# Eight of eleven pairs through seven products of sums in the down projection, and weight sums by accumulating transfers

## The chip, the cores and the metric

The kernel runs on one core of a Trainium2 chip. The metric is the device time of one execution in microseconds (us), smaller is better; of the kernel before there are three runs, with a median of 1926.14 us (1925.88 to 1926.17).

## The reference

The program is a trunk of two encoder layers on x of 512 tokens by 1024 channels, in float32. Each layer is a half-weighted SwiGLU feed-forward block (FFN), a mixer of four attention groups, and a second such FFN, each followed by a residual sum and a layer norm.

```python
def _swiglu(h, w_gu, w_down):
    gate, up = jnp.split(h @ w_gu, 2, axis=-1)
    return (jax.nn.silu(gate) * up) @ w_down

for l in range(DEPTH):                      # DEPTH = 2
    x = _layer_norm(alpha * x + 0.5 * _swiglu(x, ffn_w_gu[l, 0], ffn_w_down[l, 0]), ...)
    mix = _token_mixers(x, ...)
    x = _layer_norm(alpha * x + mix, ...)
    x = _layer_norm(alpha * x + 0.5 * _swiglu(x, ffn_w_gu[l, 1], ffn_w_down[l, 1]), ...)
```

The hidden width D_FF is 2816, so gate and up together are a 1024 x 5632 matrix and the down projection is 2816 x 1024. The change touches the FFN alone, which runs four times.

## The kernel before

**Float32 by three matmuls.** TensorE (PE) multiplies numbers rounded to a shorter format (fp32r). Each operand is therefore split into a high half (a cast, on ScalarE, ACT) and a low half (operand minus high half, on VectorE, DVE). Each product then takes three matmuls: high by high, high by low, low by high. In the names, `wh` and `wl` are the halves of weights, `al` those of the input, `dh` and `hh`/`hl` those of hidden values. So each weight tile costs a cast on ACT and a subtraction on DVE (line 405 for gate/up, line 542 for the down weights, line 239 for whole rows of down weights).

**Gate and up by seven products.** The hidden width is cut into 11 pairs of 256 columns. For each pair the product of x (tokens in two halves, channels in two halves) with the weights (channels in two halves, gate and up) is a 2 x 2 by 2 x 2 block product, and it is computed with seven block products of sums, not eight of blocks (class `Pair`). Step names go by product: 1, 2, 5, 6, 7, 3, 4, in this order. The four 512 KB weight tiles of a pair are b11, b21, b12, b22 (first digit: channel half; second: gate or up). DVE forms the weight sums in place: line 458 b11 += b12 (step 5), line 468 b11 + b22 (step 6), line 476 b12 += b22 (step 7), line 491 b21 += that of step 6 (step 4). Each product is 24 matmuls of 256 columns into the banks ga, gb, gc. The results of the activation, h0 (tokens 0 to 255) and h1 (256 to 511), stay in SBUF.

**Down projection by seven products.** Class `Unit` takes two pairs at a time, for which the down weights are four blocks d11, d21, d12, d22 (first digit: pair; second: half of the output columns), each two tiles of 256 KB. It also does seven products, in the order 1, 2, 5, 3, 6, 7, 4, each 12 matmuls of 512 columns into the banks da, db, dc. After each, DVE adds the two banks to x (line 556). Sums of weights are formed on DVE (line 524, two operations of 512 columns each), and so are sums of h (lines 569, 574, 575, 581). `UNITS` says how many units there are: three, so six pairs. Their 21 steps are interleaved with the gate/up steps of pairs 3 to 10 of the program.

**The other pairs directly.** The ten 128-row chunks of the remaining five pairs are multiplied directly, 24 matmuls of 512 columns for each chunk, into eight `acc` banks. The last four chunks (`TAIL`) go token block by token block, so that the layer norm of one block runs beside the matmuls of the next.

**Queues and buffers.** All loads are issued by SP in one queue (line 96). POOL (GpSimd) has no work in the FFN but a power in the layer norm (line 334). A scheduling layer (Tile) orders the instructions of each engine, so the order of a queue isn't that of the code. Weight halves have four buffers each (`WB`); the tiles of down weights have ten (`hl`).

Of the kernel before, what the change touches and what calls it, by code (L numbers as in the profile page):

```python
# [15 lines left out]
ALU = mybir.AluOpType  # L16
AX = mybir.AxisListType
PSUM = bass.MemoryType.PSUM
P = 128
DM = 1024  # L20
S = 512
NT = S // P
DEPTH = 2
FF = 2816
NC = FF // P
# [5 lines left out]
FD = DM // 2  # L31
# [42 lines left out]
def tile_encoder(ctx: ExitStack, tc: tile.TileContext, d: dict, out: bass.AP):  # L74
    nc = tc.nc
    ve, se, ge, te = nc.vector, nc.scalar, nc.gpsimd, nc.tensor

    def pool(name, bufs=1, **kw):
        return ctx.enter_context(tc.tile_pool(name=name, bufs=bufs, **kw))

    cst, st, raw, whi, wlo, blk, sm = (pool("cst"), pool("state"), pool("raw"), pool("whi"), pool("wlo"),
                                       pool("blk"), pool("small"))
    ps = pool("ps", 2, space=PSUM)
    RAW, WB = 3, 4
    BUFS = {"v": 8, "st": 8, "kr": 1, "hl": 10, "nat": 4, "tb": 3, "o": 2, "od": 1, "o2": 2, "p": 6, "oT": 8}
    NPT = 4
    LAG = 3

# [9 lines left out]
    def block(tag, name, dt=F32, width=512):  # L98
        return blk.tile([P, width], dt, tag=tag, name=name, bufs=BUFS[tag])

# [141 lines left out]
    def unit_rows(src, lo=None):  # L242
        r = raw.tile([P, DM], F32, tag="r", name="wr", bufs=RAW)
        load(r, src)
        return wsplit(r, DM, lambda a: a, lo)
# [16 lines left out]
    def cols_of(w):  # L262
        return w.rearrange("(k p) f -> p k f", p=P)

    def mm(o, a, b, start, stop, **kw):
        te.matmul(o, a, b, start=start, stop=stop, **kw)  # L266
        n = 1
        for w in b.shape[1:]:
            n *= w
        pe[0] += n / 2400.0  # L270
# [98 lines left out]

    HTAGS = ["oT"] * 4 + ["nat"] * 2 + ["tb"] + ["v"] * 2 + ["oT"] * 2  # L370
    PARTS = {6: "p", 7: "oT", 8: "p", 9: "nat", 10: "v"}
    UNITS = 3
    TMP = ["o", "o", "od", "o2", "o2", "kr"]

    def ffn(l, f, last, to_next, early=("p", "nat")):
        wgu = cols_of(d["ffn_w_gu"][l, f])
        wd = d["ffn_w_down"][l, f]
        ring = {"raw": 0, "tmp": 0}
        v3 = lambda t: t.rearrange("p (c t) -> p c t", c=2)
# [2 lines left out]
        def raw_tile(name):  # L382

            ring["raw"] += 1
            if ring["raw"] % 7 in (1, 3, 5):
                return raw.tile([P, DM], F32, tag="r", name=name, bufs=RAW)
            return blk.tile([P, DM], F32, tag="pt", name=name, bufs=NPT)
# [5 lines left out]
        def parts4(r, early=None):  # L393

            if early is None:
                h = whi.tile([P, DM], F32R, tag="h", name="wh", bufs=WB)
                lo = wlo.tile([P, DM], F32R, tag="l", name="wl", bufs=WB)
                pieces = [(h, lo, 0, 4)]
            else:
                pieces = [(block(early, "we", F32R), block(early, "we", F32R), k0, 2) for k0 in (0, 2)]  # L400
            out_ = []
            for h, lo, k0, nk in pieces:
                q = slice(k0 * 256, (k0 + nk) * 256)
                se.copy(h, r[:, q])  # L404
                ve.tensor_tensor(lo, r[:, q], h.bitcast(F32), op=ALU.subtract)  # L405
                out_.append(tuple(w.rearrange("p (k c) -> p k c", c=256) for w in (h, lo)) + (k0, nk))
            return out_

        def product(n, o, w, first):

            for c in range(2):
                seq = []
                for h, lo, k0, nk in w:
                    for k in range(nk):
                        seq += [(h, k, k0 + k, "h"), (h, k, k0 + k, "l")]
                for h, lo, k0, nk in w:
                    for k in range(nk):
                        seq.append((lo, k, k0 + k, "h"))
                for m, (a, k, kk, hl) in enumerate(seq):
                    mm(o[:, c], a[:, k, c * P:(c + 1) * P], alk(n, hl, kk), first and c == 0 and m == 0,  # L420
                       c == 1 and m == len(seq) - 1, skip_group_check=True)

        class Pair:
# [6 lines left out]
            def load(self, ns=(11, 21, 12, 22)):  # L430
                j = self.j
                for n in ns:
                    k, u = n // 10 - 1, n % 10 - 1
                    self.r[n] = raw_tile(f"b{n}")
                    load(self.r[n].rearrange("p (k c) -> p k c", k=4),
                         wgu[:, 4 * k:4 * k + 4, u * FF + j * 256:u * FF + (j + 1) * 256])
                return self

            def bank(self, tag, name):
                return bank(tag, name).rearrange("p (c t) -> p c t", c=2)  # L440
# [32 lines left out]

            def step7(self):
                r = self.r
                ve.tensor_tensor(r[12], r[12], r[22], op=ALU.add)
                w = parts4(r[12])
                product(7, self.a, w, False)

                ve.tensor_tensor(self.p5, self.a, self.p5, op=ALU.add)  # L480
# [25 lines left out]
        class Unit:  # L506
# [6 lines left out]
            def load(self):  # L513
                for n, k, u in ((11, 0, 0), (21, 1, 0), (12, 0, 1), (22, 1, 1)):
                    self.r[n] = []
                    for q in range(2):
                        r = block("hl", "d")
                        c = 2 * (self.j + k) + q
                        load(r, wd[c * P:(c + 1) * P, u * FD:(u + 1) * FD])
                        self.r[n].append(r)  # L520
# [37 lines left out]
            def steps(self):  # L558
                (h11, h21), (h12, h22) = (tuple(t.rearrange("p c t -> p (c t)") for t in H[self.j + k]) for k in range(2))
                two = lambda tags, name: [bank(t, name) for t in tags]  # L560
                self.load()
                a = two(("pt", "pt"), "da")
                self.step(1, h11, -1.0, 11, a, True, (0, 0, -1.0))
                yield
                b = two(("pv", "pj"), "db")
                self.step(2, h12, -1.0, 21, b, True, (0, 0, -1.0))
                yield
                t = block("tb", "dt")
                ve.tensor_tensor(t, h21, h22, op=ALU.subtract)
                self.add(11, 12)  # L570
                c = two(("pv", "pj"), "dc")
                self.step(5, t, 1.0, 11, c, True, (1, 1, 1.0))
                yield
                ve.tensor_tensor(t, h11, t, op=ALU.subtract)
                ve.tensor_tensor(h12, h12, t, op=ALU.subtract)
                self.step(3, h12, 1.0, 22, c, False, (0, 1, 1.0))
                yield
                self.add(11, 22)
                self.step(6, t, 1.0, 11, a, False, (0, 1, 1.0))
                yield  # L580
                ve.tensor_tensor(h21, h21, h11, op=ALU.subtract)
                self.add(12, 22)
                self.step(7, h21, 1.0, 12, a, False, (1, 1, 1.0))
                yield
                self.add(21, 11)
                self.step(4, h22, -1.0, 21, a, False, (1, 0, -1.0))
                yield
# [31 lines left out]
        for step in p1.rest():  # L619
            step()  # L620
        down_steps = itertools.chain.from_iterable(Unit(2 * u).steps() for u in range(UNITS))
        done = 0
        for j in range(2, NB):
            p = Pair(j).load()
            for n, step in enumerate([p.step1, p.step2] + p.rest()):
                step()
                if j > 2:
                    k = 7 * (j - 3) + n + 1
                    while done < 7 * UNITS and done * (7 * (NB - 3) - 2) < k * 7 * UNITS:
                        next(down_steps)  # L630
# [26 lines left out]
        def down(t, c, w, ns=range(2)):  # L657
            wh, wl = w
            hh, hl = h_of(c, t)
            for n in ns:  # L660
                sl = slice(n * FD, (n + 1) * FD)
                mm(acc[t][n], hh, wh[:, sl], c == 4 * UNITS, False)
                mm(acc[t][n], hl, wh[:, sl], False, False)
                mm(acc[t][n], hh, wl[:, sl], False, c == NC - 1)

        for c in range(4 * UNITS, NC - TAIL):
            w = unit_rows(wd[c * P:(c + 1) * P])
# [991 lines left out]
    for l in range(DEPTH):  # L1659
        ffn(l, 0, False, (new_xT, to_xT), ("p", "oT" if l else "nat"))  # L1660
        mixer(l)
        ffn(l, 1, l == DEPTH - 1, (norm_to_al,) if l < DEPTH - 1 else None)
# [24 lines left out]
```

## Time and profile before

| | before |
|---|---|
| median of three runs | 1926.14 us |
| profiled execution | 1928.49 us, of which the span 1926.7 us |
| mean granted TensorE clock | 0.988 |
| instructions | 32397 |
| PE, DVE, ACT, POOL busy | 97%, 88%, 55%, 13% of the span |
| bytes moved by DMA | 205.65 MB |

The profile is that of one execution. "Busy" is the time in which an engine had an instruction under way; neighbouring instructions overlap by some 80 ns on DVE and by more on PE, so what an instruction costs in a full queue is the distance between the starts of two neighbours. In a row of the timeline stand the start, the length, the engine, the line, the operation, output and inputs, and, in brackets, the idle time ahead of it with what ended it. PEld is the loading of weights into PE. In a row of one line's instructions, the three numbers are the shortest, the median and the longest duration in ns.

### The profile page before, as it was taken

The numbers are of one execution on the slowest core, as the hardware profiler recorded it, in microseconds if no ns is written. First come the engines' busy times: TensorE is split into PE (matmuls) and PEld (weight loads), VectorE is DVE, ScalarE is ACT, GpSimd is POOL, SyncE is SP. The second block draws the span as 40 slices with busy tenths as digits, with TensorE's granted clock in tenths as the row PEclk, the third lists the DMA queues.
The fourth block names the chain that finished last, engine by engine and source line by source line (L and its number), as shares of the span: only waits on it lengthen the run. The fifth ranks groups of instructions, "written<-read, shape, count | busy, mean of one in ns | idle before, by whom it ended". The sixth has DMA issues, their size and how long they took to land.

```text
span 1926.7 us, 32397 instructions
## 1 busy us (share of the span) xinstructions
PE 1875.4 (97%) x12252; PEld 1704.4 (88%) x12252; DVE 1696.6 (88%) x2739; ACT 1061.6 (55%) x1851; POOL 251.6 (13%) x381
## 2 busy tenths in 40 slices
PE   7999999999999999999999999999999989999998
PEld 7999998888887899999789999988887879999996
DVE  7999995858988999999599999958689989999975
ACT  5555554248776645555375555532587865455551
POOL 0000000245731000000000000002467300000001
PEclk9999999999999999999999999999999999999999
DMA  6333314243343424233342333241533335144221
GB/s 231 107 121 108 102 52 136 81 121 99 93 105 110 138 94 131 84 104 112 108 133 80 106 99 121 65 144 52 144 92 84 102 110 170 50 132 131 64 91 66
DMA packets 164701, 205.65 MB, mean 107 GB/s; under 512 B 15360, under 2 KB 123904, under 8 KB 164544
## 3 DMA queue, kind: packets, MB, share of 16 engines
q1 hardware_dynamic: 164544, 203.57, 34.3%
q8 instruction: 97, 1.59, 0.3%
q14 instruction: 60, 0.49, 0.1%
HBM read 178.49 MB, written 2.10 MB: 94 GB/s over the span
## 4 chain that ended last, share of the span: by engine, by line
PE 63%; DVE 9%; ACT 2%; POOL 1%; DMA 1%; issue 1%; SPq 0%; DVEq 0%; POOLq 0%; ACTq 0%
PE ga L266 19%; PE gc L266 9%; PE acc L266 7%; PE da L266 5%; PE gb L266 4%; PE nat L266 3%; PE sc L266 3%; PE dc L266 3%; PE pjt L266 2%; PE ptb L112 2%; PE pv L266 2%; PE db L266 1%; DVE p L766 1%; DMA b<-in_ffn_w_gu_dram 1%; PE op L266 1%
## 5 line engine op out<-in xcount | busy, mean ns | idle before, releaser
L404 ACT CAST wh<-b 128x1024 fp32r<-128x1024 f32 x292 | 303.8, 1051 | 255.2 <-DVE b L468 61.1
L266 PE MATMUL ga<-al,wh 128*128 128x256 f32 x2752 | 389.7, 284 | 2.9 <-DVE al L179 1.7
L266 PEld LDWEIGHTS ga<-al,wh 128*128 128x128 f32 x2752 | 357.2, 191 | 14.2 <-ACT u L472 7.0
L405 DVE TENSOR_TENSOR wl<-b,wh 128x1024 fp32r<-128x1024 f32 x292 | 351.8, 1217 | 3.3 <-ACT wh L404 3.0
L266 PE MATMUL ga<-al,wl 128*128 128x256 f32 x1376 | 222.4, 284 | 5.4 <-DVE wl L405 5.3
L334 POOL TENSOR_TENSOR rs<-rs,mhalf 128x1 f32<-128x1 f32 x24 | 21.6, 901 | 1457.0 <-DVE rs L333 1449.0
L266 PE MATMUL gc<-al,wh 128*128 128x256 f32 x1408 | 203.5, 286 | 6.5 <-ACT al L178 5.1
L266 PEld LDWEIGHTS ga<-al,wl 128*128 128x128 f32 x1376 | 190.4, 193 | 6.4 <-DVE wl L405 6.4
L266 PEld LDWEIGHTS gc<-al,wh 128*128 128x128 f32 x1408 | 187.2, 195 | 9.5 <-ACT al L178 5.5
L541 ACT CAST wh<-d 128x512 fp32r<-128x512 f32 x168 | 98.5, 619 | 87.8 <-PE ga L266 39.2
L239 DVE TENSOR_TENSOR wl<-wr,wh 128x1024 fp32r<-128x1024 f32 (+2 forms) x50 | 59.4, 1188 | 78.5 <-ACT wh L238 78.5
L266 PE MATMUL acc<-wl,hh 128*128 128x512 f32 x320 | 125.3, 392 | 0.2 <-DVE wl L239 0.2
L266 PE MATMUL acc<-wh,hl 128*128 128x512 f32 x320 | 125.0, 390 | 0.0
L266 PE MATMUL acc<-wh,hh 128*128 128x512 f32 x320 | 124.9, 390 | 0.0
L266 PE MATMUL gc<-al,wl 128*128 128x256 f32 x704 | 117.0, 286 | 1.3 <-DVE wl L405 1.3
L238 ACT CAST wh<-wr 128x1024 fp32r<-128x1024 f32 (+2 forms) x50 | 50.9, 1025 | 121.9 <-PE acc L266 76.1
L542 DVE TENSOR_TENSOR wl<-d,wh 128x512 fp32r<-128x512 f32 x168 | 109.7, 683 | 0.1
L266 PE MATMUL da<-wh,dh 128*128 128x512 f32 x384 | 103.9, 392 | 0.0
L266 PEld LDWEIGHTS gc<-al,wl 128*128 128x128 f32 x704 | 99.6, 195 | 1.7 <-DVE wl L405 1.7
L808 ACT CAST pth<-ptb 128x512 fp32r<-128x512 f32 (+2 forms) x128 | 69.7, 545 | 43.0 <-PE ptb L112 41.9
L266 PE MATMUL gb<-al,wh 128*128 128x256 f32 x640 | 90.7, 285 | 0.0
L811 DVE TENSOR_TENSOR ptl<-ptb,pth 128x512 fp32r<-128x512 f32 (+2 forms) x128 | 80.6, 630 | 7.0 <-ACT pth L808 6.6
(323 smaller groups left out, 4157.9 us busy)
## 6 DMA issues: line engine op xcount, KB each, us to landing
b<-in_ffn_w_gu_dram SPq DMA_DIRECT2D x176, 512.0 KB, 4.6
d<-in_ffn_w_down_dram SPq DMA_DIRECT2D x96, 256.0 KB, 3.5
wr<-in_ffn_w_down_dram SPq DMA_DIRECT2D x40, 512.0 KB, 3.3
wr<-in_w_in_dram SPq DMA_DIRECT2D x30, 512.0 KB, 3.8
k<-ph SPq DMA_DIRECT2D x64, 128.0 KB, 2.3
wr<-in_w_out_dram SPq DMA_DIRECT2D x16, 512.0 KB, 3.2
qs<-ph SPq DMA_DIRECT2D x32, 128.0 KB, 2.4
ln_g<-in_ln_g_dram SPq DMA_DIRECT2D x14, 256.0 KB, 3.8
```

The lines of the kernel that those rows point to most:

```text
L112: te.transpose(o, a, ident)
L238: se.copy(h[:, w], r[:, w])
L239: (lo or ve).tensor_tensor(l[:, q], r[:, q], h[:, q].bitcast(F32), op=ALU.subtract)
L266: te.matmul(o, a, b, start=start, stop=stop, **kw)
L334: ge.tensor_tensor(rs[:, 1:2], rs[:, 0:1], mhalf[:, 0:1], op=ALU.pow)
L404: se.copy(h, r[:, q])
L405: ve.tensor_tensor(lo, r[:, q], h.bitcast(F32), op=ALU.subtract)
L541: se.copy(wh[:, sl], self.r[rn][q])
L542: ve.tensor_tensor(wl[:, sl], self.r[rn][q], wh[:, sl].bitcast(F32), op=ALU.subtract)
L766: ve.tensor_tensor_reduce(p, sb, nd, -h.slope, h.sink[0] if h.sink else 3.0e38, ALU.add, ALU.min, m)
L808: se.copy(b.ph, b.tb[:, b.k0:b.k1])
L811: ve.tensor_tensor(b.pl, b.tb[:, b.k0:b.k1], b.ph.bitcast(F32), op=ALU.subtract)
```

## The change

Four things change.

- `UNITS` goes from 3 to 4. Pairs 6 and 7 now also pass the down projection by seven products; the direct part keeps six chunks, two ahead of the tail. The 28 down steps are spread over the same gate/up steps of pairs 3 to 10.
- The weight sum of step 7 is taken from DVE in nine of the eleven pairs of each FFN (not in the first two), and in all units. POOL issues a transfer from DRAM with `accum_op=ALU.add`, which adds the weights of b22 (or d22) to the tile b12 (or d12).
- The gate/up weights lie in DRAM as whole tiles (128 x 1024, contiguous); before, a load gathered pieces of 256 columns (1 KB).
- The space for descriptors of transfers that POOL issues (`dynamic_dma_scratch_size`) goes from 256 to 1024 bytes, and the tiles of down weights from ten to nine.

```diff
-    BUFS = {"v": 8, "st": 8, "kr": 1, "hl": 10, "nat": 4, "tb": 3, "o": 2, "od": 1, "o2": 2, "p": 6, "oT": 8}
+    BUFS = {"v": 8, "st": 8, "kr": 1, "hl": 9, "nat": 4, "tb": 3, "o": 2, "od": 1, "o2": 2, "p": 6, "oT": 8}
...
-    UNITS = 3
+    UNITS = 4
...
-        wgu = cols_of(d["ffn_w_gu"][l, f])
+        wgu = d["ffn_w_gu"][l, f]
...
                     self.r[n] = raw_tile(f"b{n}")
-                    load(self.r[n].rearrange("p (k c) -> p k c", k=4),
-                         wgu[:, 4 * k:4 * k + 4, u * FF + j * 256:u * FF + (j + 1) * 256])
+                    load(self.r[n], wgu[j, u, k])
...
             def step7(self):
                 r = self.r
-                ve.tensor_tensor(r[12], r[12], r[22], op=ALU.add)
+                if self.j < 2:
+                    ve.tensor_tensor(r[12], r[12], r[22], op=ALU.add)
+                else:
+                    ge.dma_start(r[12], wgu[self.j, 1, 1], accum_op=ALU.add)
                 w = parts4(r[12])
                 product(7, self.a, w, False)
...
                 ve.tensor_tensor(h21, h21, h11, op=ALU.subtract)
-                self.add(12, 22)
+                for q in range(2):
+                    c = 2 * (self.j + 1) + q
+                    ge.dma_start(self.r[12][q], wd[c * P:(c + 1) * P, FD:], accum_op=ALU.add)
                 self.step(7, h21, 1.0, 12, a, False, (1, 1, 1.0))
...
-    nc = _bacc.Bacc("TRN2", target_bir_lowering=False, num_devices=1, dynamic_dma_scratch_size=256)
+    nc = _bacc.Bacc("TRN2", target_bir_lowering=False, num_devices=1, dynamic_dma_scratch_size=1024)
...
+    wgu = given["ffn_w_gu"].reshape(DEPTH, 2, 2, 4, P, 2, NC // 2, 256).transpose(0, 1, 6, 5, 2, 4, 3, 7)
+    given["ffn_w_gu"] = np.ascontiguousarray(wgu).reshape(DEPTH, 2, NC // 2, 2, 2, P, DM)
```

Lines behind the change move by three to five (458 becomes 457, 542 becomes 545). The first place at which the order differs is DVE's queue in the first FFN at its third pair, from the sum of step 5 (b11_683 += b12_687) to the low half of step 7 (wl_817, made from b12_687). Before:

```order
L458 TENSOR_TENSOR b11_683<-b11_683,b12_687 128x1024
L487 TENSOR_TENSOR u2_586<-gc_529,u2_586 128x512
L476 TENSOR_TENSOR b12_687<-b12_687,b22_689 128x1024
L496 TENSOR_TENSOR h0_677<-s1_326,u2_586 128x512
L405 TENSOR_TENSOR wl_754<-b11_683,wh_753 128x1024
L500 TENSOR_TENSOR h1_681<-s2_679,p5_554 128x512
L468 TENSOR_TENSOR b11_683<-b11_683,b22_689 128x1024
L535 SCALAR_TENSOR_TENSOR dh_1056<-h0_677,dh_1055 128x512
L491 TENSOR_TENSOR b21_685<-b21_685,b11_683 128x1024
L405 TENSOR_TENSOR wl_786<-b11_683,wh_785 128x1024
L454 TENSOR_TENSOR s1_720<-gb_726,s1_720 128x512
L405 TENSOR_TENSOR wl_817<-b12_687,wh_816 128x1024
```

Now, from the same sum to the same low half:

```order
L457 TENSOR_TENSOR b11_683<-b11_683,b12_687 128x1024
L490 TENSOR_TENSOR u2_586<-gc_529,u2_586 128x512
L499 TENSOR_TENSOR h0_677<-s1_326,u2_586 128x512
L405 TENSOR_TENSOR wl_754<-b11_683,wh_753 128x1024
L538 SCALAR_TENSOR_TENSOR dh_1024<-h0_677,dh_1023 128x512
L503 TENSOR_TENSOR h1_681<-s2_679,p5_554 128x512
L467 TENSOR_TENSOR b11_683<-b11_683,b22_689 128x1024
L572 TENSOR_TENSOR dt_1110<-h1_518,h1_681 128x512
L494 TENSOR_TENSOR b21_685<-b21_685,b11_683 128x1024
L405 TENSOR_TENSOR wl_786<-b11_683,wh_785 128x1024
L453 TENSOR_TENSOR s1_720<-gb_726,s1_720 128x512
L405 TENSOR_TENSOR wl_817<-b12_687,wh_816 128x1024
```

The sum b12_687 += b22_689 is gone from this queue, and a difference of two h (dt) has moved up; ten operations still stand between the first and the last row. The second place is POOL's queue from the program's start to the first layer norm (rs, line 334). Before, after the constants:

```order
L1673 MEMSET const-float32-1.0 128x1
L1673 MEMSET const-bfloat16-1.0 128x1
L1673 MEMSET const-uint8-127 128x1
L1683 UNCONDITIONAL_BRANCH
L334 ISA
L334 TENSOR_TENSOR rs_3630<-rs_3630,mhalf_84 128x1
```

Now, after the same branch, the first of seventeen transfers of this FFN:

```order
L1691 UNCONDITIONAL_BRANCH
L479 DMA b12_687<-in_ffn_w_gu_dram 128x1024
L479 DMA b12_914<-in_ffn_w_gu_dram 128x1024
L587 DMA d_957<-in_ffn_w_down_dram 128x512
L587 DMA d_959<-in_ffn_w_down_dram 128x512
L479 DMA b12_1265<-in_ffn_w_gu_dram 128x1024
L587 DMA d_1575<-in_ffn_w_down_dram 128x512
L479 DMA b12_1613<-in_ffn_w_gu_dram 128x1024
L587 DMA d_1577<-in_ffn_w_down_dram 128x512
```

They stand in the order in which their tiles come due; the nine of pairs and the eight of units alternate in one queue, ahead of the power of the layer norm.

## The prediction

> **What bounds the kernel now.** I read the page's first two parts first. TensorE (PE) is busy nearly all the time, and so is VectorE (DVE) over long stretches; GpSimd (POOL) has nothing to do outside the attention stage.
>
> ```profile
> PE 1875.4 (97%) x12252; PEld 1704.4 (88%) x12252; DVE 1696.6 (88%) x2739; ACT 1061.6 (55%) x1851; POOL 251.6 (13%) x381
> PE   7999999999999999999999999999999989999998
> ```
>
> ```profile
> DVE  7999995858988999999599999958689989999975
> POOL 0000000245731000000000000002467300000001
> ```
>
> A share over the span hides which engine waits for which, so next I took the busy times by stage: in the first feed-forward block (FFN) the stretch in which gate/up steps alternate with down steps (91 to 303 us), then its direct down projection with the layer norm's start (303 to 340 us); and most of the second FFN (650 to 870 us).
>
> ```profile
> 91.32:302.57 211.25, 211.25 (x1538) 200.39 (x1537) 202.18 (x261) 111.41 (x154) 0.00 (x0) 1.00 0.31 99
> 302.57:340.00 37.43, 37.43 (x167) 30.95 (x166) 16.94 (x27) 14.97 (x21) 0.00 (x0) 1.00 0.43 134
> ...
> 650.00:870.00 220.00, 219.29 (x1622) 209.09 (x1622) 216.00 (x275) 113.87 (x157) 0.00 (x0) 1.00 0.33 104
> ```
>
> The columns are length, then busy us of PE, PEld, DVE, ACT, POOL, granted clock, DMA share, GB/s. PE has no gap in either part of the first FFN and 0.7 us in 220 in the second; DVE fills 95.7% and 98.2% of that time. So PE sets the pace, and DVE follows with 9 us and 4 us to spare per FFN. In the direct part DVE is busy for less than half. The table of waits says the same: over the whole run the weight loads of the largest product group waited 6.4 us for low halves of weights.
>
> ```profile
> PEld ga L266 <- DVE wl L405: 6.4, 5, 2.3
> ```
>
> A saved matmul is therefore saved time, as long as DVE's extra work stays below PE's time and no new wait stands in front of either.
>
> **The change, part by part.** *PE.* "Busy" of one matmul (284 or 390 ns) overlaps its neighbours, so I price by the distance of starts in PE's timeline.
>
> ```profile
> 85.70 1.09 PE L266 MATMUL da<-wh,dh 128*128 128x512 f32 x4
> ...
> 88.44 1.11 PE L266 MATMUL gb<-al,wh 128*128 128x256 f32 x8
> ...
> 91.32 1.12 PE L266 MATMUL gc<-al,wh 128*128 128x256 f32 x8
> ...
> 303.73 0.39 PE L266 MATMUL acc<-wl,hh 128*128 128x512 f32 x1
> ...
> 317.56 0.39 PE L266 MATMUL acc<-wh,hh 128*128 128x512 f32 x1
> ```
>
> A down step (12 matmuls) takes 88.44 - 85.70 = 2.74 us, a gate/up product (24) 2.88 us; in the direct part 61 matmuls lie between 303.73 and 317.56, 0.2267 us each. Per FFN the fourth unit adds 7 x 2.74 = 19.2 us, and four chunks fewer (4 x 24 = 96 matmuls) take away 21.8 us: 2.6 us saved, 10.3 us over four FFNs.
>
> [...]
>
> *DVE.* Here too distances count, not durations.
>
> ```profile
> 188.86 0.69 DVE L556 SCALAR_TENSOR_TENSOR x<-dc,x 128x512 f32<-128x512 f32 x1
> 189.46 1.28 DVE L542 TENSOR_TENSOR wl<-d,wh 128x512 fp32r<-128x512 f32 x2
> 190.66 1.22 DVE L458 TENSOR_TENSOR b<-b,b 128x1024 f32<-128x1024 f32 x1
> 191.80 0.68 DVE L487 TENSOR_TENSOR u<-gc,u 128x512 f32<-128x512 f32 x1
> ```
>
> A 512-wide operation takes 0.60 us, a 1024-wide one 1.14 us. A unit had 47 operations of 512 (14 weight halves, 7 halves of sums of h, 14 additions to x, 12 other sums); without the two of step 7 it has 45, 27.0 us. Per FFN the alternating stretch gains 27.0 us, loses 3 x 2 x 0.60 = 3.6 us of the older units and 9 x 1.14 = 10.3 us of step 7 of nine pairs: +13.1 us for DVE beside +19.2 us for PE. So DVE goes to 215.3 of 230.4 us in the first FFN (93.4%) and 229.1 of 239.2 us in the second: its spare time grows to 15 and 10 us. The direct part loses 4 x 1.14 + 4 x 0.60 = 7.0 us: 9.9 us of DVE beside 37.4 - 21.8 = 15.6 us of PE. I cost DVE at nothing; what hides it is PE's own gapless work.
>
> *The accumulating transfers.* Per FFN nine of 512 KB and eight of 256 KB, issued by POOL. Each waits for the sum of step 5, which still reads the old half; behind it on POOL stand only the next such transfers, in the order of their sums. ScalarE's (ACT's) cast, then DVE's low half, wait for the landing, with everything behind them on those queues. The third pair of the first FFN has the shortest time for it.
>
> ```profile
> 59.35 1.22 DVE L458 TENSOR_TENSOR b<-b,b 128x1024 f32<-128x1024 f32 x1
> ...
> 69.17 2.35 DVE L405 TENSOR_TENSOR wl<-b,wh 128x1024 fp32r<-128x1024 f32 x2
> ```
>
> ```profile
> 75.28 1.22 PE L266 MATMUL ga<-al,wh 128*128 128x256 f32 x8
> ```
>
> ```profile
> L404 ACT CAST wh<-b 128x1024 fp32r<-128x1024 f32 x292 | 303.8, 1051 | 255.2 <-DVE b L468 61.1
> ```
>
> Before, step 7's low half begins 69.17 - 60.57 = 8.6 us after step 5's sum, and PE starts that product at 75.28: DVE is 6 us ahead of it. In the new DVE order 10 operations (8.2 us) stand between that sum and that low half; the other pairs of the first two FFNs have 8.7 to 15.4 us, a unit's 256 KB over 25 us. Less the cast of 1.05 us, a transfer may take 7.1 us where it is tightest. No row has such a transfer; the nearest are plain loads of the same size.
>
> ```profile
> L96 SPq DMA_DIRECT2D b<-in_ffn_w_gu_dram x176: 367/368/1388, 2.1 to 1822.2; - x176
>   DMA to landing us min/median/max: 3.3/4.6/9.7
> ```
>
> It takes 3.3 us or more; above, the row's maximum is 9.7 us. It moves three streams (source, old and new contents) where a load moves two: 1.5 x 4.6 = 6.9 us is my value, and costs nothing.
>
> *The rest.* Gate/up loads become 4 KB rows in place of 1 KB: off the path, except perhaps in the opening, where the DMA engines are full (share 1.07) and PE sits idle for 3.78 us behind x.
>
> ```profile
> 10.00:20.00 10.00, 10.00 (x71) 10.00 (x70) 6.72 (x11) 7.65 (x14) 0.00 (x0) 1.00 1.07 400
> ```
>
> ```profile
> 29.59 0.58 PE L266 MATMUL gc<-al,wh 128*128 128x256 f32 x1 [3.78 <-ACT al L178]
> ```
>
> I give it 0 (between 0 and -3.8 us). The ninth-for-tenth tile of the down weights costs nothing: b22 of a unit comes free at step 6's sum, one step sooner. SP issues eight loads of 256 KB in place of four of 512 KB per FFN, the same bytes. ACT gains 14 weight casts and 7 of h and loses 8, at 53% busy.
>
> *Sum.* 1926.1 - 10.3 = 1915.8 us as median. The profiled execution took 1928.5 us with a span of 1926.7; the same execution should show a span near 1916.5.
>
> **The rivals.** *Late transfers (slower).* If a 512 KB accumulate takes T, DVE stops for T + 1.05 minus its window. With the second FFN's nine windows (8.7, 10.0, 8.8, 11.2, 13.6, 11.2, 11.2, 9.4, 11.8 us) that is 7 us at T = 10, 14 us at 11, 22 us at 12, against 10 us spare plus the 2.6 us saved: it decides from T of about 10.8 us, just over the load's maximum of 9.7. T = 12 would give 12 us lost per FFN, 48 - 10 = +38: 1964 us. For it speaks that nothing here shows such a transfer; against it that most loads take half of that. Chance 0.09.
>
> *POOL in DVE's way.* The attention stage shows both engines hold each other up now and then.
>
> ```profile
> L785 POOL TENSOR_SCALAR p<-p,l x96: 480/696/1347, 416.1 to 1538.6; 128x512 f32<-128x512 f32 x64, 128x256 f32<-128x256 f32 x16, 128x384 f32<-128x384 f32 x16
> ```
>
> ```profile
> L931 DVE TENSOR_TENSOR wl<-wr,wh x68: 665/683/1000, 393.9 to 1548.5; 128x512 fp32r<-128x512 f32 x68
> ```
>
> POOL loses up to 0.65 us (1347 - 696), DVE up to 0.32 us, at the median nothing. Seventeen issues at 0.32 us are 5.4 us of DVE, inside the 10 spare. From (10 + 2.6)/17 = 0.74 us each the gain is gone; at a whole 1.14 us each, 19.4 - 10 = 9.4 us per FFN, 1953 us. Chance of about no change by this 0.07, of slower 0.04.
>
> The Trainium skill (SBUF — State Buffer, SBUF: two separate sides) speaks against the change: a DMA issued from GpSimd has its descriptors written by that engine, which a VectorE operation in a two-port mode locks out; it reports about 620 ns growing to 3100 ns. By that, T would be some 2.5 us longer, 9.4 us, still under 10.8. No run so far shows a descriptor being written.
>
> *Half the gain.* Only two direct chunks (10.9 us of PE) are left between the last gate/up step and the tail; if DVE enters them late, 1 to 2 us per FFN come back: 1920 to 1922 us. Against it stands 9.9 of 15.6 us. Chance 0.13.
>
> **How the numbers follow.** About 0.2%, 3.9 us, is what a measurement of this kernel can tell from no change. Forecast 0.67, half the gain 0.13, no change 0.07, slower 0.13: faster 0.80, same 0.07, slower 0.13. The range goes from 1912.0 (the opening's 3.8 us) to 1924.0, which takes in the lost half and leaves out the upper end of "no change" and the slower cases.
>
> **What would show it.** Right: PE still without gaps in the FFNs, 48 matmuls fewer; DVE near 94% there and 24 us busier in all; 68 transfers issued by POOL that land in 5 to 9 us; hardly any wait of ACT's cast of b12 for a DMA. Wrong: landing beyond 10 us, DVE operations longer than 683 and 1217 ns in the FFNs, or PE waiting for wl in each pair.

## The result and the profile after

The changed kernel takes 1913.29 us (median of 4 runs, 1911.3 to 1913.82), the kernel before 1926.01 us on the same chip (4 runs, 1925.83 to 1926.17). The ratio is 0.9933 (95% interval 0.9919 to 0.9948): 12.7 us faster, where 10.3 were forecast. The profiled execution took 1913.15 us with a span of 1911.4.

The busy times of the profile after, in the order of those shown of before:

```profile
PE 1859.7 (97%) x12204; PEld 1691.3 (88%) x12204; DVE 1724.2 (90%) x2827; ACT 1081.9 (57%) x1903; POOL 310.2 (16%) x449
```

PE has 48 matmuls fewer. DVE is 27.6 us busier and POOL 58.6: it now carries the 68 issues. The same stages as before (the first FFN's alternating stretch, its direct part, most of the second FFN), in the columns known from the prediction:

```profile
90.77:320.66 229.89, 229.89 (x1623) 215.91 (x1621) 218.51 (x293) 122.02 (x174) 11.28 (x13) 1.00 0.44 126
320.66:342.93 22.27, 22.19 (x99) 17.96 (x97) 16.16 (x29) 10.35 (x16) 1.00 (x1) 1.00 0.61 174
646.00:886.00 240.00, 240.00 (x1734) 227.26 (x1733) 234.40 (x308) 126.42 (x178) 13.95 (x16) 1.00 0.49 136
```

PE has no gap in the alternating stretches (second column), and now none in the second FFN either; DVE is busy 95.0% and 97.7% there, about the shares of before (95.7% and 98.2%).

Where the time came from is read from PE's timeline, by the first matmul of the direct part (acc, 512 wide) and the first transposition for the next stage (xtp). Before:

```profile
302.57 0.40 PE L266 MATMUL acc<-wh,hh 128*128 128x512 f32 x1
...
346.45 0.66 PE L112 MATMUL xtp<-ident,x 128*128 128x128 f32 x4
```

After, with the first down step of the FFN, which before began at 85.70:

```profile
85.15 1.09 PE L266 MATMUL da<-wh,dh 128*128 128x512 f32 x4
...
320.66 0.40 PE L266 MATMUL acc<-wh,hh 128*128 128x512 f32 x1
...
342.93 0.66 PE L112 MATMUL xtp<-ident,x 128*128 128x128 f32 x4
```

The direct part fell from 43.88 to 22.27 us: 21.6 us less, against 21.8 forecast. The stretch ahead of it, from the first down step, grew from 216.87 to 235.51 us: 18.6 us more, against 19.2 forecast. That is 3.0 us saved in the first FFN, in place of 2.6.

In the other three FFNs there is one thing more. Before, PE's steps did not all follow each other without delay. In the second FFN a gate/up product that usually takes 2.88 us took 3.75 (759.69 to 763.44):

```profile
759.69 1.21 PE L266 MATMUL ga<-al,wh 128*128 128x256 f32 x8 [0.19 <-ACT wh L404]
761.43 0.74 PE L266 MATMUL ga<-al,wl 128*128 128x256 f32 x4 [0.52 <-DVE wl L405]
762.00 1.11 PE L266 MATMUL ga<-al,wh 128*128 128x256 f32 x8
762.96 0.64 PE L266 MATMUL ga<-al,wl 128*128 128x256 f32 x4
763.44 0.86 PE L266 MATMUL da<-wh,dh 128*128 128x512 f32 x3
```

PE waits for a low half (0.52 us at 761.43), and on both sides of the wait the matmuls start later than their rhythm. DVE's queue just ahead of it, before:

```profile
752.95 1.22 DVE L476 TENSOR_TENSOR b<-b,b 128x1024 f32<-128x1024 f32 x1
754.09 0.68 DVE L454 TENSOR_TENSOR s<-gb,s 128x512 f32<-128x512 f32 x1
...
759.02 1.22 DVE L491 TENSOR_TENSOR b<-b,b 128x1024 f32<-128x1024 f32 x1
760.15 2.35 DVE L405 TENSOR_TENSOR wl<-b,wh 128x1024 fp32r<-128x1024 f32 x2
```

Line 476 is a sum of step 7, and it stands 7 us ahead of the low half that comes late. Outside the first steps of each FFN, five steps are late in the profile of before: by 0.34 and 0.86 us in the second FFN (starts 756.48 and 759.69), 0.35 in the third (1105.82), and 0.34 and 0.86 in the fourth (1708.81 and 1712.03), 2.75 us in all. In the profile after there is no such step.

The transfers, from the answers for lines 479 (pairs) and 587 (units), with their sizes on the page:

```profile
b<-in_ffn_w_gu_dram POOLq DMA_DIRECT2D x36, 512.0 KB, 5.2
d<-in_ffn_w_down_dram POOLq DMA_DIRECT2D x32, 256.0 KB, 4.0
```

```profile
L479 POOL DMA_DIRECT2D b<-in_ffn_w_gu_dram x36: 842/863/1038, 60.7 to 1843.7; - x36
...
  ACT wh L404: 1.1, 1
...
DMA to landing us min/median/max: 5.0/5.2/8.0
```

They land in 5.2 us (at most 8.0) where 6.9 were forecast; ACT's cast waits for them once, for 1.1 us. An issue keeps POOL for 0.86 us. It starts a little after the sum that it waits for: the sum at 660.24 ends at 661.46, the issue stands at 662.11, 0.65 us later. So from sum to landing it is 5.9 us here; over all 36 pairs the median is 5.8 us (5.5 to 8.7). The bracket in the second row below names the operation behind the sum, which had ended as well; but the issue stands 0.64 or 0.65 us behind the sum in 24 of the 36 places, also where the next operation on DVE was still running, and 0.36 to 0.59 us in the others.

```profile
660.24 1.22 DVE L457 TENSOR_TENSOR b<-b,b 128x1024 f32<-128x1024 f32 x1
```

```profile
662.11 0.95 POOL L479 DMA_DIRECT2D b<-in_ffn_w_gu_dram  x1 [45.80 <-DVE x L364]
```

DVE's operations have not become longer beside them (min/median/max in ns):

```profile
L405 DVE TENSOR_TENSOR wl<-b,wh x292: 1209/1217/1227, 14.1 to 1860.0; 128x1024 fp32r<-128x1024 f32 x146
```

### The profile page after: what moved, and what is told of

Its sections match the earlier page's. It is cut to its first block, busy times and chain, and to the rows that moved or that the text cites. A ratio compares the mean times of both kernels' runs of the same rounds, so it can differ in the third digit from the quotient of the medians.

```text
span 1911.4 us, 32788 instructions
## 1 busy us (share of the span) xinstructions
PE 1859.7 (97%) x12204; PEld 1691.3 (88%) x12204; DVE 1724.2 (90%) x2827; ACT 1081.9 (57%) x1903; POOL 310.2 (16%) x449
## 4 chain that ended last, share of the span: by engine, by line
PE 83%; DVE 10%; POOL 2%; DMA 2%; ACT 2%; issue 2%; SPq 0%; DVEq 0%; POOLq 0%; ACTq 0%
PE ga L266 26%; PE gc L266 13%; PE da L266 9%; PE gb L266 6%; PE acc L266 5%; PE dc L266 5%; PE nat L266 4%; PE sc L266 3%; PE db L266 2%; PE pjt L266 2%; PE pv L266 2%; PE ptb L112 2%; PE op L266 1%; DVE p L771 1%; DMA b<-in_ffn_w_gu_dram 1%
## 5 line engine op out<-in xcount | busy, mean ns | idle before, releaser
L544 ACT CAST wh<-d 128x512 fp32r<-128x512 f32 x224 | 133.6, 619 | 145.3 <-PE ga L266 73.7
L479 POOL DMA_DIRECT2D b<-in_ffn_w_gu_dram x36 | 31.4, 872 | 768.5 <-DVE h L503 190.2
L545 DVE TENSOR_TENSOR wl<-d,wh 128x512 fp32r<-128x512 f32 x224 | 150.2, 683 | 1.3 <-ACT wh L544 0.7
L266 PE MATMUL da<-wh,dh 128*128 128x512 f32 x512 | 138.5, 392 | 0.0
L266 PEld LDWEIGHTS da<-wh,dh 128*128 128x128 f32 x512 | 91.7, 189 | 15.7
L559 DVE SCALAR_TENSOR_TENSOR x<-da,x 128x512 f32<-128x512 f32 x128 | 87.4, 685 | 2.9 <-PE da L266 1.6
L790 POOL TENSOR_SCALAR p<-p,l 128x512 f32<-128x512 f32 (+2 forms) x96 | 65.6, 688 | 139.9 <-DVE l L789 98.1
L266 PEld LDWEIGHTS gb<-al,wh 128*128 128x128 f32 x640 | 84.6, 193 | 1.6
L266 PE MATMUL da<-wl,dh 128*128 128x512 f32 x256 | 79.1, 390 | 0.0
```

Source lines behind the costliest of these rows:

```text
L479: ge.dma_start(r[12], wgu[self.j, 1, 1], accum_op=ALU.add)
L544: se.copy(wh[:, sl], self.r[rn][q])
L545: ve.tensor_tensor(wl[:, sl], self.r[rn][q], wh[:, sl].bitcast(F32), op=ALU.subtract)
L559: ve.scalar_tensor_tensor(xs, banks[i], sign * 0.5 * INV_A, xs, op0=ALU.mult, op1=ALU.add)
L790: ge.tensor_scalar(b.p[0], b.p[0], l[:, 3:4], 1.0, op0=ALU.mult, op1=ALU.mult)
```

## The experiments

Every ratio below is to the kernel before, run on the same chip. The theory: PE sets the pace, and the gain is its 48 saved matmuls; DVE's time is worth nothing as long as it stays below PE's; the transfers give it that time and cost nothing while they land early enough. Two questions lay beside it: what brought the 2.4 us over the forecast, and where the transfers would begin to cost.

**The parts of the change apart.** Four kernels: the fourth unit alone (before, with `UNITS = 4`); the transfers and the layout alone (after, with `UNITS = 3`); the layout alone; and the change without the layout, where the transfer reads rows of 1 KB and 2048 bytes of scratch replace 1024:

```
-                    ge.dma_start(r[12], wgu[self.j, 1, 1], accum_op=ALU.add)
+                    ge.dma_start(r[12].rearrange("p (k c) -> p k c", k=4),
+                                 wgu[:, 4:8, FF + self.j * 256:FF + (self.j + 1) * 256], accum_op=ALU.add)
```

> The kernel before with the fourth unit alone: step 7's sums stay on DVE, the gate/up weights keep their old layout. Theory (the transfers pay for the unit): in the first FFN of the profile after, DVE is busy 218.5 of 229.9 us from 90.8 to 320.7 us; step 7's sums of nine pairs and four units put 9 x 1.14 + 8 x 0.60 = 15.1 us back, 233.6 us in 229.9, and in the second FFN 268.8 + 15.1 = 283.9 in 279.3 us. DVE then sets the pace by some 4 us per FFN, 2 of which its 6 us of spare time in the direct part cannot give back to a PE that has already stood: 1920 to 1930 us, and PE waits for low halves of weights (before: 6.4 us in all) grow past 15 us. Rival (the transfers are idle decoration, PE alone decides): 1913 to 1915 us and no more such waits than before.

> The changed kernel with three units as before: transfers and new layout stay. Theory (PE sets the pace, and DVE's freed time is worth nothing by itself): the 12 matmuls per FFN come back, 1913.3 + 4 x 2.97 = 1925.2 us, within 0.1% of the kernel before. Rival (DVE's wait in front of PE's weight loads, 6.4 us over the run before, was worth money): 1920 to 1923 us.

> The kernel before with the gate/up weights alone laid out so that a block is read in rows of 4 KB. The measured gain is 12.7 us where the matmules were priced at 10.3. Theory (the opening's earlier start of 0.55 us is all the layout brings, the rest lies in the matmuls): 1925.4 to 1926.1 us. Rival (the layout brings the 2.4 us over): 1923.5 to 1924.0 us.

> The changed kernel with the old layout of the gate/up weights; the accumulating transfers read rows of 1 KB. Theory (transfers have time to spare): they land later than the 5.2 us of the profile after, but below 9 us, and the time is 1913.3 + 0.5 = 1913.8 us. Rival (transfers of 1 KB rows land past 10.8 us, where the prediction put the point at which DVE stops): 1918 us or more, with waits of ACT's casts for these transfers of several us per FFN.

The kernel before took 1925.66 us beside them. The fourth unit alone: 1933.65 us, ratio 1.0040 (1.0026 to 1.0054). Without the transfers the unit makes the kernel slower, by more than was expected, and the place is the one foreseen:

```profile
734.11 1.21 PE L266 MATMUL ga<-al,wh 128*128 128x256 f32 x8
736.48 0.75 PE L266 MATMUL ga<-al,wl 128*128 128x256 f32 x4 [1.16 <-DVE wl L405]
...
738.92 0.73 PE L266 MATMUL da<-wh,dh 128*128 128x512 f32 x2 [0.27 <-ACT wh L541]
```

This product takes 4.81 us in place of 2.88. From the first down step to the direct part the four FFNs need 236.0, 241.0, 240.5 and 241.0 us, against 235.5, 235.4, 235.4 and 235.4 after: 16.7 us of the 20 that lie between the two kernels. The rival, that PE alone decides, is out.

The transfers alone: 1922.28 us, 0.9984 (0.9975 to 0.9992). Here the theory falls and the rival holds: there is a gain of 3.1 us (1.5 to 4.8) without a saved matmul, and in this profile the five late steps of before are gone. So there is a gain beside the saved matmuls, and this is its place. The layout alone: 1925.77 us, 1.0001 (0.9992 to 1.0009), nothing, with the same five late steps. The change without the layout: 1914.01 us, 0.9937 (0.9924 to 0.9949), as fast as with it, though its transfers land in 6.1 us (median) rather than 5.2. So the layout brings nothing in time.

**Which of the transfers are needed.** In the changed kernel, step 7's sums of the pairs or of the units went back to DVE:

```
-                    ge.dma_start(r[12], wgu[self.j, 1, 1], accum_op=ALU.add)
+                    ve.tensor_tensor(r[12], r[12], r[22], op=ALU.add)
```

```
-                    ge.dma_start(self.r[12][q], wd[c * P:(c + 1) * P, FD:], accum_op=ALU.add)
+                self.add(12, 22)
```

> The changed kernel with the sums of step 7 of the pairs back on DVE; the units keep their transfers. DVE gets 9 x 1.14 = 10.3 us per FFN: 268.8 + 10.3 = 279.1 of 279.3 us in the second FFN, 228.8 of 229.9 in the first. Theory of balance (a wait appears only where DVE's sum passes PE's): just at the edge, 1914 to 1918 us. Rival (single places run short before the sum does, as with 2.4 us of late steps before, at 96 to 98%): 1920 to 1928 us, with late gate/up steps in each FFN.

> The changed kernel with the sums of step 7 of the units back on DVE; the pairs keep their transfers. DVE gets 8 x 0.60 = 4.8 us per FFN: 273.6 of 279.3 us in the second FFN. Theory of balance: nothing, 1913 to 1914 us. Rival (single places): 1915 to 1919 us.

Pairs on DVE: 1918.2 us (1912.4 to 1918.33), 0.9948 (0.9934 to 0.9962). The interval of the ratio overlaps that of the full change, so the time alone decides nothing; its profile shows steps that are late by 0.83 us in the second and fourth FFN, and the stretches from first down step to direct part are 1.9, 0.5 and 1.9 us longer than after in the last three FFNs, 4.3 us. Units on DVE: 1912.42 us, 0.9928 (0.9916 to 0.9941), no late step behind the opening. So 32 of the 68 transfers do nothing for the time, 36 some 4 us by the profile, and both together 20 (1933.65 less 1913.3). The two prices do not add up, because DVE's time costs little until its sum comes near PE's, and then about all that goes beyond. In the second FFN DVE is busy 268.8 of PE's 279.3 us after (from 646 us to the direct part); 4.8 us more make 98% of that, 10.3 us 99.9%, 15.1 us 101.6%, and the stretch grows by nothing, 1.9 and 5.6 us. The edge isn't sharp: before, two steps of that FFN were late at 98.2%.

**How late a transfer may be.** In each of the nine pairs POOL issues plain loads into the same tile ahead of the accumulating transfer: one of 64 columns, one of the whole tile, or two of the whole tile. The transfer waits for them.

```
+                    ge.dma_start(r[12][:, :64], wgu[self.j, 1, 0][:, :64])
                     ge.dma_start(r[12], wgu[self.j, 1, 1], accum_op=ALU.add)
```

```
+                    ge.dma_start(r[12], wgu[self.j, 0, 1])
                     ge.dma_start(r[12], wgu[self.j, 1, 1], accum_op=ALU.add)
```

The second diff, and the third kernel, which issues that load twice, read another block of the same size (w21) than the expectations say, so that step 7's products there use a sum other than the reference's; the bytes and the waits are the ones meant.

> The changed kernel; in each of the nine pairs, POOL first loads the old half into the same tile once more, after step 5's sum, and only then issues the accumulating transfer: the sum arrives later by about a load (4.2 us), at 5.2 + 4.2 = 9.4 us, 10 us with the wait between. Theory (DVE runs ahead of PE, so a late sum is paid only when all the stops of an FFN exceed DVE's spare time; the point was put at 10.8 us): 1913 to 1916 us, DVE's and ACT's waits in the pairs grow by some 7 us per FFN. Rival (DVE has no lead left where it stops, each stop is PE's too): 7 us in each of four FFNs, 1935 to 1945 us.

> As the run with one reload, with two reloads ahead of each of the nine transfers: about 5.2 + 2 x 4.2 = 13.6 us, 14 with the waits. Theory: above the point. Stops of 14 + 1.05 less the windows of 8.7 to 13.6 us are 39 us in the second FFN, less some 10 to 13 us of spare time: 26 us per FFN, 1913 + 4 x 26 = 2017 us as an upper end; a fifth of that, 1930 us, if the transfers overlap other pairs' work. Rival (the sums are due much later than DVE's order says, because ACT and DVE can take other work first): below 1918 us.

> The changed kernel; in each of the nine pairs POOL first loads 64 of the 1024 columns of the old half into the same tile once more, then issues the accumulating transfer. From the end of step 5's sum to the landing: 0.65 us to the issue, about 2.5 for the small load, 5.4 for the transfer, 8.5 us in place of 5.9. Theory (as the prediction put it: DVE's windows of 8.7 to 13.6 us in the second FFN, spare time of 10 us): stops of about 2 us per FFN, hidden: 1913 to 1914 us. Rival (what stands behind the waiting cast on ACT, the copies out of the accumulators, is due at once, so that a stop is PE's after a us or two): 1915 to 1920 us.

The small load: 1913.71 us, 0.9937 (0.9924 to 0.9949), no cost, though ACT's casts now wait 19.2 us in 13 places for the transfers. By POOL's timeline the transfer is issued 2.36 us after the small load (690.15 and 692.51), so the sum lands 0.65 + 2.36 + 5.2 = 8.2 us after step 5's. One whole load: 1931.68 us, 1.0034 (1.0022 to 1.0046), between the two expectations; issued 3.86 us later (695.21 and 699.07), landing at 0.65 + 3.86 + 5.4 = 9.9 us. Two: 2045.0 us, 1.0618 (1.0598 to 1.0639), 28 us above the upper end that was expected; issued 8.15 us later (726.24 and 734.39), landing at 0.65 + 8.15 + 7.0 = 15.8 us. Over all 36 pairs the medians from sum to landing are 8.2, 10.0 and 15.7 us. So the edge lies between 8.2 and 10.0 us, not at 10.8. (These are typical values: six of the 36 transfers in the run with the small load landed after 9.7 us or more, the last after 10.9, and cost nothing where they stood.) What happens there stands on three queues of the run with one whole load. ACT:

```profile
737.67 1.05 ACT L404 CAST wh<-b 128x1024 fp32r<-128x1024 f32 x1 [3.63 <-DMA b<-in_ffn_w_gu_dram]
738.62 0.58 ACT L462 COPY p<-gc 128x512 f32<-128x512 f32 x1
...
742.12 0.58 ACT L471 COPY u<-ga 128x512 f32<-128x512 f32 x1
```

DVE:

```profile
738.75 1.23 DVE L405 TENSOR_TENSOR wl<-b,wh 128x1024 fp32r<-128x1024 f32 x1 [3.45 <-ACT wh L404]
739.89 0.68 DVE L560 SCALAR_TENSOR_TENSOR x<-da,x 128x512 f32<-128x512 f32 x1
740.49 0.68 DVE L539 SCALAR_TENSOR_TENSOR dh<-h,dh 128x512 fp32r<-128x512 f32 x1
741.09 0.69 DVE L560 SCALAR_TENSOR_TENSOR x<-da,x 128x512 f32<-128x512 f32 x1
```

PE:

```profile
737.85 0.64 PE L266 MATMUL ga<-al,wl 128*128 128x256 f32 x4
740.72 1.48 PE L266 MATMUL da<-wh,dh 128*128 128x512 f32 x4 [2.23 <-DVE x L560]
742.76 0.51 PE L266 MATMUL ga<-al,wh 128*128 128x256 f32 x2 [0.56 <-ACT u L471]
```

PE does not wait for the late weights. It waits for its accumulators: the addition to x that empties da stands behind the waiting low half on DVE, and the copy that empties ga behind the waiting cast on ACT. These are due a step earlier than the weights. In the third FFN the longest wait, 4.27 us at 1090.84, is for the high half of a sum of h (dh, line 538), which ACT also makes behind a waiting cast. From first down step to direct part, no wait of PE in this profile is for a half of gate/up weights.

**More of the same.** Three kernels beyond the change. One has a fifth unit, whose seven steps go beside the last seven gate/up steps, and two direct chunks (`UNITS = 5`, `TAIL = 2`, and `while done < (min(28, -(-k * 28 // 49)) if k < 50 else k - 21)` as the rule of the order). One has that and also the sums of step 5 in the pairs and of steps 5 and 6 in the units by transfers; in its pairs both transfers (steps 5 and 7) are issued behind step 1, and that of step 5 takes w21 in place of w12. One is the changed kernel with the additional transfers in the units alone:

```
+                self.more(11, 0, 1)
+                self.more(12, 1, 1)
                 yield
...
-                self.add(11, 12)
...
+                self.more(11, 1, 1)
                 yield
...
-                self.add(11, 22)
```

Here `more(o, k, u)` issues the two accumulating transfers of one weight block, and stands behind steps 1 and 5; in the third kernel the second line stands ahead of step 7.

> The changed kernel with a fifth unit (pairs 8 and 9), spread so that 28 down steps go beside the first 49 gate/up steps and seven beside the last seven; two direct chunks are left. Theory (PE sets the pace only while DVE has time): PE loses another 3 us per FFN, but DVE gets 25.8 us more beside 18.6 us of PE, on top of 268.8 of 279.3 in the second FFN, and the last seven steps hold 7 x (2.88 + 2.74) = 39.3 us of PE against some 41 us of DVE: 1913 to 1925 us, and PE waits for low halves. Rival (PE alone): 1901 to 1903 us.

> Five units, and also the sums of step 5 (pairs and units) and of step 6 (units) by accumulating transfers: in each of nine pairs and five units DVE loses one 1024-wide or four 512-wide sums, 9 x 1.14 + 5 x 2.4 = 22 us per FFN. Theory (DVE's time is what a unit costs, transfers are free while they land in time): DVE needs about 224 of PE's 249 us, PE stays ahead nowhere, 1902 to 1907 us with what the shorter direct part loses at the end. Rival (the transfers of step 5, due two gate/up steps after step 1, come too late, or POOL's queue holds them up in order): 1915 to 1940 us, with waits of DVE's second sums and ACT's casts for DMAs.

> The changed kernel, and in the four units also the sums of steps 5 and 6 by accumulating transfers of 256 KB, which have some 15 us of time: DVE loses 16 x 0.60 = 9.6 us more per FFN. Theory (PE alone sets the pace now, DVE's time is worth nothing any more): 1913 to 1914 us. Rival (DVE's 96% still costs PE a little, or the direct part starts earlier): 1908 to 1911 us. Third: 16 more transfers in POOL's order delay the pairs' transfers, 1915 us and more.

Five units: 1948.34 us, 1.0120 (1.0106 to 1.0134), outside both expectations. The stretch from the first down step to the direct part is 19.0 to 19.1 us longer than after in every FFN, PE's own time for seven steps (7 x 2.74 = 19.2), with no late step: DVE was not what failed. From the start of the direct part to the first keys of the attention it takes 66.5 us, against 76.9 after, 10.4 us less where PE lost 21.8 us of work. The windows of that place in the run with five units:

```profile
340.00:360.00 20.00, 17.45 (x77) 13.16 (x75) 19.64 (x40) 5.69 (x10) 2.77 (x3) 0.93 0.12 42
360.00:380.00 20.00, 18.16 (x67) 13.91 (x68) 16.08 (x32) 5.76 (x10) 1.95 (x4) 0.73 0.34 82
```

After, in the same place:

```profile
340.00:360.00 20.00, 19.92 (x100) 16.24 (x99) 19.70 (x38) 5.78 (x9) 2.91 (x3) 1.00 0.10 29
360.00:380.00 20.00, 20.00 (x96) 16.70 (x95) 15.01 (x37) 5.35 (x10) 6.64 (x10) 1.00 0.37 105
```

With two chunks of direct work left, the layer norm (DVE busy 19.64 of 20 us) has no cover: PE stands still for 4.4 us, and its granted clock falls to 0.93 and 0.73, a loss of 20 x 0.07 + 20 x 0.27 = 6.8 us, 5.7 of them while PE was busy (by the rows of 4 us in the last section). Together that is 10.1 of the 11.4 us that did not come. So the first FFN is 19.04 - 10.36 = 8.7 us longer than after. The others, taken in the same way to the first step of what follows, are 4.1, 7.9 and 6.0 us longer. These 26.7 us are most of the 35 by which this kernel is slower than the changed one; the two attention stages are 8.6 us longer in its profile, and why was not followed.

Five units with more transfers: 1980.23 us, 1.0286 (1.0272 to 1.03). The pairs' transfers land in 7.6 us (median; at most 11.3) and ACT's casts wait 52.0 us for them in 14 places. The mechanism of the rival holds, but the time lies 40 us above its range, because its loss came on top of the 35 us of the five units. The additional transfers in the units alone: 1912.96 us, 0.9932 (0.9920 to 0.9944). DVE is 37 us less busy than after (1687.0 us) and the time is the same. No version beats the changed kernel by more than can be measured.

## Why the prediction was right, point by point

**PE, 10.3 us.** The mechanism holds, and the term was somewhat too small. The direct part lost 21.6 us (forecast 21.8) and the unit cost 18.6 (19.2): 3.0 us in the first FFN in place of 2.6. A down step between two gate/up steps takes 2.75 us, as forecast. But before, three gate/up steps of this stretch are cut in two, ten matmuls ahead of the next step and fourteen behind it:

```profile
99.82 1.12 PE L266 MATMUL gc<-al,wh 128*128 128x256 f32 x8
100.78 0.40 PE L266 MATMUL gc<-al,wl 128*128 128x256 f32 x2
101.17 1.22 PE L266 MATMUL ga<-al,wh 128*128 128x256 f32 x8
...
104.14 0.40 PE L266 MATMUL gc<-al,wl 128*128 128x256 f32 x2
104.38 1.12 PE L266 MATMUL gc<-al,wh 128*128 128x256 f32 x8
```

The two steps take 6.0 us together (99.82 to 105.82), where two uncut ones take 5.76; the others begin at 210.99 and 293.72. That is 0.7 us, and after, no gate/up step is cut.

**What was left out: late steps.** The prediction took PE to be without gaps and put the fewer sums on DVE at nothing, although its own row showed 219.29 of 220.00 us in the second FFN. The idle time of that row is less than the loss: the two late steps there cost 1.2 us, because a product that waits for weights also starts its neighbouring matmuls late. The run with the transfers alone shows 3.1 us (1.5 to 4.8) for it.

**How the terms add up.** That 10.3 us and the late steps come out near the 12.7 us measured is in part luck. In the profiles the four FFNs, each taken from its first down step to the first step of what follows (the keys of the attention, the next FFN's first down step, the end), are 3.0, 3.6, 3.2 and 4.2 us shorter after than before: 14.1 us. With the transfers alone they are 1.9 us shorter than before, so 12.2 us are the unit's, where 10.3 were forecast. The medians show 1.4 us less than these 14.1 us. The change leaves the two attention stages as they were, and they take between 578 and 584 us in the profiles with three and four units, so a difference of 1.4 us cannot be followed here and stays open. The spans of the two profiled executions lie 15.3 us apart, since the one of before was 2.4 us above its median.

**DVE, 24 us busier, with room.** It is 27.6 us busier. The shares came out higher than 93.4% and 95.8% (95.0% and 97.7%: in the first FFN 218.5 us for 215.3); why was not followed. The claim that DVE's extra work is hidden holds with a narrow margin: 4.8 us more per FFN cost nothing, 10.3 us bring late steps, 15.1 us turn the gain into a loss.

**The transfers.** 6.9 us was too much; 5.2 us, 5.9 with POOL's start. The sizing by streams (1.5 times a load's 4.6) failed: the accumulating transfer takes 1.24 times the plain load of the same profile (4.2 us).

**Late transfers (0.09).** It did not come to pass, with 2.3 us to spare, as the small load shows. But the step that gave its point failed. It set DVE's stops against DVE's spare time of the whole FFN (10 us), which put the point at 10.8 us; in the run at 10 us, where it allowed 7 us of stops without harm, the stretches from first down step to direct part grew by 0.6, 3.9, 6.9 and 3.9 us. Spare time far from a stop does not help it, and what is due first behind the waiting cast is not the weights but the emptying of an accumulator, or a half of h. Had every transfer taken as long as the load's slowest (9.7 us, 10.35 with POOL's start), the forecast would have been wrong.

**POOL in DVE's way (0.11).** The low halves take 1217 ns in the middle and 1227 at most with 68 issues in the run, 1216 and 1228 before. Nothing of it shows. The Trainium skill (SBUF — State Buffer, SBUF: two separate sides) would have had the descriptors wait for a VectorE in a two-port mode; here the issues last 0.84 to 1.04 us and the transfers land in 5.0 to 8.0 us, beside a VectorE that is busy 95% of the time with operations of two sources, so no run here shows that case.

**Half the gain (0.13).** Not here, but the mechanism is real: in the run with five units, 11.4 us of the 21.8 us of PE's work that its first FFN saves in the direct part do not come, and 6.7 to 10.6 us in the others; in the first the rows show a tail that is too short to cover the layer norm. Six direct chunks are enough, two are not.

**The opening (0 to 3.8 us).** Nothing, as the layout alone shows.

## What to carry to other kernels

When two engines run at 95% beside each other, saved work on the first is worth its time only if the second gets time too: here the fourth unit cost 8 us without the transfers (1933.65 against 1925.66) and saved 9 to 10 with them (1913.29 against 1922.28; ratio 0.9933 against 0.9984). A late operand is priced by what stands behind the waiting instruction on its queue, above all by the copies that empty accumulators, and not by the spare time of the engine over a stage. And a share of work that is shifted out of a stage's end must leave enough there to cover what follows.

## What the hardware showed

An accumulating transfer of 512 KB from memory into a tile took 5.2 us to its landing (5.0 to 8.0) and one of 256 KB 4.0 us, in a run where plain loads of these sizes took 4.2 and 3.3 us (medians); with rows of 1 KB in place of 4 KB it took 6.1 us. A plain load of 32 KB that POOL issues ahead of it took 2.0 us.

In the run with five units the granted clock falls to one half after a stretch in which PE was busy for 2.10 of 4 us, and returns when it has been busy again:

```profile
352.00:356.00 4.00, 2.10 (x11) 1.36 (x9) 4.00 (x9) 0.00 (x0) 0.99 (x1) 1.00 0.00 0
356.00:360.00 4.00, 3.35 (x10) 1.76 (x9) 4.00 (x9) 1.17 (x2) 0.78 (x1) 0.63 0.00 0
360.00:364.00 4.00, 2.79 (x10) 2.16 (x11) 3.21 (x6) 1.17 (x2) 0.15 (x1) 0.50 0.02 4
364.00:368.00 4.00, 3.37 (x8) 2.17 (x8) 4.00 (x11) 0.00 (x0) 0.71 (x1) 0.50 0.19 18
368.00:372.00 4.00, 4.00 (x16) 3.20 (x15) 3.00 (x5) 0.00 (x0) 0.21 (x1) 0.66 0.38 127
372.00:376.00 4.00, 4.00 (x21) 3.18 (x20) 2.95 (x6) 3.45 (x6) 0.00 (x0) 1.00 0.38 99
```

The Trainium skill (TensorE: Matmul & The Clock Gate, Part 1: The HAM clock gate) describes a clock that is halved after an idle window of about 3.4 us. The halving agrees with 0.50; but here the only gap of PE ahead of the fall is 1.90 us long, as the row at 355.45 shows, so a whole window without work was not needed:

```profile
355.45 1.29 PE L112 MATMUL xtp<-ident,x 128*128 128x128 f32 x8 [1.90 <-DVE x L327]
```

In the 40 us from 340 to 380, 4.4 us of idle time went with 6.8 us of lost clock, 5.7 of them while PE was busy.
